# Gathered-row products behind the U chunk and behind the V chunk of each step

## The chip, the cores and the metric

The kernel runs on one core of a Trainium2 chip. The time is that of one execution on the device in microseconds (us); of several executions the median is taken. The engines are TensorE (PE in the profile; PEld is its weight load), VectorE (DVE), ScalarE (ACT), GpSimd (POOL) and SyncE (SP, used here only to issue transfers). Each works through its own queue in order.

## The reference

One layer of a decoder over 512 tokens of width 1024: layer norm, a mixer of state-space heads and latent attention, layer norm, then a product-key expert layer ("PEER"), and a last layer norm. Only the expert layer matters here. For each token it picks 128 of 16384 experts (8 heads x 16) and gives each a gate; then

```python
u = jnp.take(u_table, expert_idx, axis=0)
act = jax.nn.gelu(jnp.einsum('td,thkd->thk', xb, u).astype(jnp.float32), approximate=False)
v = jnp.take(v_table, expert_idx, axis=0)
return jnp.einsum('thk,thkd->td', (gate * act).astype(xb.dtype), v)
...
h = layer_norm(DEEPNORM_ALPHA * h + ffn, ln_ffn_g[l], ln_ffn_b[l])
```

Everything is float32.

## The kernel before

**Two ways through the expert layer.** For the first 384 tokens the kernel doesn't gather: it multiplies all 16384 experts with all tokens and lets a matrix of gates, zero where an expert wasn't picked, select. The tables are cut into 128 chunks of 128 experts. (For 64 of the 384 the first half is done by gathering too, earlier, and comes in ready.) The last block of 128 tokens is gathered: for each of the 128 picks s of a token one indirect transfer on POOL brings 128 rows, one per token (512 KB), of the u table, and VectorE multiplies them with the token's vector and sums (the *product* of step s < 128, line 1548); after GELU and gate (lines 1550 and 1552) the same is done with the v table, where VectorE adds the scaled row to a sum (128 <= s < 256, line 1554). So 256 products run on VectorE beside the matmuls of the other tokens.

**U chunk and V chunk.** `u_chunk` (line 1413; `u_half`, line 1395) computes the 320 activations of one chunk: 24 matmuls (line 85 to 87: high x high, high x low, low x high halves of the float32 values), then GELU on ScalarE into `ACT` (line 1406). `v_chunk` (line 1674) first makes the low half `Pl` of the next chunk's weights (`v_lo`, line 1659), prepares the chunk after next (`v_prep`: one quarter of a gate load on SP, line 1595; activations times gates, line 1628 on VectorE, or copies on ScalarE, lines 1631 and 1632), splits off its high half `Ph` (line 1651), and runs 18 matmuls into six accumulators (lines 1668, 1669, 1672).

**The stream of tables.** Both kinds of chunk take a 512 KB weight tile from one stream, `win` (class `Stream`, line 93), in turn U, V, U, V. An `item()` for chunk n of the stream emits, for the chunk n + 3, the high half on ScalarE (`wih`, every fourth in a buffer of its own, `wihx`; line 122), for n + 2 the low half on VectorE (`wil`, line 132), and behind that the load of the raw tile n + 5 on SP (line 104), which takes the buffer that this low half has just read. There are three raw buffers.

**The order of the work** is written out by hand (line 1698 on). A *step* is one turn of this loop. For `vc` 0 to 8 a step holds a V chunk alone; for `vc` 9 to 52 it holds a U chunk (`uc` 84 to 127) and a V chunk; for 53 to 120 again a V chunk alone. The last seven V chunks are kept for the end.

**Dealing out the products.** `gather` (line 1517) is a generator; each turn fetches the row of s + 4 on POOL and emits product s on VectorE, and notes s in `GS[0]`. There are five row buffers, so the row of s + 4 takes the buffer of product s - 1. At the end of each step the loop works out `want`, the count of products that should stand by then, from the units of chunk work that are left (`units`, line 1696: a V chunk is 0.86, a U and a V chunk together 2), and pumps the generator until it is reached (lines 1715 to 1719). `GS[1]` and `GS[2]` hold the units and the count when this began, in step 0. So on VectorE a step with both chunks is: `wil` for the next U chunk, `Pl`, line 1628 where there is one, `wil` for the next V chunk, then three or four products.

Of the kernel before, what the change touches and what calls it, by code (L numbers as in the profile page):

```python
# [46 lines left out]
T_U = 3.6  # L47
T_Q = 6.3
ROWS = 5
ENDU = 11  # L50
GP = 4
WV = 0.86
GST = (1, 3, 5, 7)
LOWA = (*range(2, 32, 2), 34, 38)
# [12 lines left out]
def tile_block(ctx: ExitStack, tc: tile.TileContext, I, out):  # L67
# [6 lines left out]
    def pool(name, bufs=1, **kw):  # L74
        p = tc.alloc_tile_pool(name=name, bufs=bufs, **kw)
        opened.append(p)
        return p
# [11 lines left out]
    def chain(*gs):  # L89
        for g in gs:  # L90
            yield from g
# [188 lines left out]
    def item():  # L280
        cnt[0] += 1
        return win.get(cnt[0] - 1)
# [749 lines left out]
    def stage1(m):  # L1032
        yield top16(sc.pop(m), 128, TV4[:, :, m], TI4[:, :, m])
        h = m // 2
        if m % 2:
            cand = rt.tile([128, NB, 88], F32, name="cand")
            for c0, a0, na, w in ((0, 0, 1, 16), (16, 1, 3, 8), (40, 4, 12, 4)):
                sh = [128, NB, na, w]
                (V if m == 15 else G).tensor_tensor(
                    cand[:, :, c0:c0 + na * w].rearrange("p h (a b) -> p h a b", a=na),  # L1040
                    TV4[:, :, m - 1, a0:a0 + na, None].to_broadcast(sh),
                    TV4[:, :, m, None, 0:w].to_broadcast(sh), op=OP.add)
            late_c.append((cand, h))
        if late_c and (m % 2 == 0 or m == 15):
            cand, h = late_c.pop()
            yield (0.7 if m == 15 else 0.0) + top16(cand, 88, TS4[:, :, h], PO4[:, :, h])
# [267 lines left out]
    def pump(g, us):  # L1314
        bal[0] = min(bal[0] + us, us)
        while bal[0] > 0:
            c = next(g, None)
            if c is None:
                bal[0] = 0.0
                return False  # L1320
            bal[0] -= c
        return True
# [61 lines left out]
    def refill():  # L1384
        while away:
            t = act_tile()
            if t is None:
                return
            c = away.pop(0)
            G.dma_start(t, asp[c - KEEP])  # L1390
            ACT[c] = t
# [21 lines left out]
    def u_chunk(c, psum=None):  # L1413
        for e in range(2):
            u_half(c, e, psum)
# [54 lines left out]
    fill = iter(())  # L1470
    for m in range(17):
# [6 lines left out]
        if m:  # L1478
            fill = chain(fill, stage1(m - 1))
# [35 lines left out]
    GS = [-1, 0, 0]  # L1515

    def gather():
        close(ijp)
        x3 = UR["x3"]
        gp3 = pool("gp3", side="right")  # L1520
        gp2 = pool("gp2", side="right")
        gp4 = pool("gp4", side="right")
        row = lambda s: (gp2 if s % ROWS < 3 else gp4).tile([128, D], F32, name="row", bufs=3 if s % ROWS < 3 else ROWS - 3)
        hd = gp3.tile([128, 128], F32, name="hd")
        ac = gp2.tile([128, D], F32, name="ac")
        V.tensor_scalar(wide(ac), x3, ALPHA, None, op0=OP.mult)
        R = {}
        yield 0.1

        def fetch(s):  # L1530
            if s < 256:
                R[s] = row(s)
                G.indirect_dma_start(out=R[s], out_offset=None, in_=I["u"] if s < 128 else I["v"],  # L1533
                                     in_offset=bass.IndirectOffsetOnAxis(ap=ix3[:, s % 128:s % 128 + 1], axis=0))
        for s in range(ROWS - 1):
            fetch(s)
            if s == 1:
                yield 0.0
            if s == 2:
                yield 0.0  # L1540
        for s in range(256):
            GS[0] = s
            if s == 0:
                yield 3.4
            fetch(s + ROWS - 1)
            r = R.pop(s)
            if s < 128:
                V.scalar_tensor_tensor(wide(r), wide(r), 1.0, x3, op0=OP.mult, op1=OP.mult, accum_out=hd[:, s:s + 1])  # L1548
                if s == 127:
                    A.activation(hd, hd, AF.Gelu)  # L1550
                    yield 0.2
                    V.tensor_tensor(hd, hd, g3, op=OP.mult)
            else:
                V.scalar_tensor_tensor(ac, r, hd[:, s - 128:s - 127], ac, op0=OP.mult, op1=OP.add)  # L1554
            yield 1.2
        R2 = [row(s) for s in (256, 257)]
        for i in range(2):
            row1(R2[i], 4 + i)
        yield 1.2
        mv, rs = norm_stats(gp3, ac, "lg")  # L1560
        yield 2.2
        V.scalar_tensor_tensor(ac, ac, mv[:, 0:1], R2[0], op0=OP.subtract, op1=OP.mult)
        yield 1.2
        V.scalar_tensor_tensor(ac, ac, rs, R2[1], op0=OP.mult, op1=OP.add)
        G.dma_start(out[3 * 128:, :], ac)
        yield 1.2
        close(gp4, gp2, gp3)
# [3 lines left out]
    fill = gather()  # L1571
# [19 lines left out]
    def step_g():  # L1591
        if more_g:
            q, b0, b1 = more_g.pop(0)
            m = min(b1, b0 + GP)
            nc.sync.dma_start(gt[q][:, b0:m], gsp[b0:m, :, q * 4:q * 4 + 4, :].rearrange("b j i t -> j b i t"))
            if m < b1:
                more_g.insert(0, (q, m, b1))
            elif more_g and m - b0 + more_g[0][2] - more_g[0][1] <= GP:
                step_g()
# [19 lines left out]
    def v_prep(c):  # L1619
        load_g(c // 4)  # L1620
        if c % 4 == 0:
            load_g(c // 4 + 1)
        step_g()
        a = ACT.pop(c)
        P = vst.tile([128, NT], F32, name="P", bufs=2)
        nb = open_(c)
        if nb:
            V.tensor_tensor(P[:, :nb * 32].rearrange("p (b t) -> p b t", t=32), a[:, :nb * 32].rearrange("p (b t) -> p b t", t=32),  # L1628
                            gt[c // 4][:, :nb, c % 4, :], op=OP.mult)
        if nb < ND:  # L1630
            A.activation(P[:, nb * 32:NU], a[:, nb * 32:], AF.Copy)
        A.activation(P[:, NU:].rearrange("p (b t) -> p b t", t=32), gt[c // 4][:, ND:, c % 4, :], AF.Copy)
        if c % 4 == 3:
            gt.pop(c // 4)
        prepared[0] += 1
        return P
# [11 lines left out]
    def v_hi(c, P):  # L1648
        Ph = v_sb(c, "Ph")
        for t, a, b in Ph:  # L1650
            A.activation(t, P[:, a:b], AF.Copy)  # L1651
        pend.append((c, P, Ph))

    def v_lo():
        if pend:
            c, P, Ph = pend.pop()
            Pl = v_sb(c, "Pl")
            for (t, a, b), (h, _, _) in zip(Pl, Ph):
                V.tensor_tensor(t, P[:, a:b], h, op=OP.subtract)  # L1659
            blk = lambda z: [t[:, i:i + 128] for t, a, b in z for i in range(0, b - a, 128)]  # L1660
            PP[c] = (blk(Ph), blk(Pl))
# [12 lines left out]
    def v_chunk(c):  # L1674
        v_lo()
        P = v_prep(c + 2)
        if uc == 128:
            v_hi(c + 2, P)
        hl = item()
        if uc < 128:  # L1680
            v_hi(c + 2, P)
        for b in range(3):
            v_mm(b, c, hl)
# [11 lines left out]
    more = True  # L1695
    units = lambda: (128 - uc) * 2 + WV * (uc - vc)
    fin = None
    while vc <= LASTC:
        w = 1.0
        if uc == 128 and not win.place:  # L1700
            i0 = len(items) - 127 + LASTC
            xv = [XT[:, 2 * j:2 * j + 2].rearrange("p a b -> p (a b)") for j in range(8)]
            win.place = {i0 + j: (xv[2 * j], xv[2 * j + 1]) for j in range(4)}
        refill()
        if uc < 128 and vc >= GAP:
            u_chunk(uc)
            uc += 1
            w = 2.0
        v_chunk(vc)
        vc += 1  # L1710
        if GS[0] < 0:
            more = pump(fill, 2.1 * w)
        else:
            if not GS[1]:
                GS[1:] = units() - ENDU, GS[0]
            left = units()
            want = 253 - max(0.0, (256 - GS[2]) * (left - ENDU) / GS[1])
            while more and GS[0] < want:
                more = pump(fill, 0.1)
            if more and left < ENDU:  # L1720
                more = pump(fill, 1.8)
            if not more and fin is None:
                fin = pool("fin", side="right")
                R2 = fin.tile([128, 2, D], F32, name="R2")
                for i in range(2):
                    row1(R2[:, i], 4 + i)
                xr = [fin.tile([128, D], F32, name=f"xr{b}") for b in range(3)]
                for b in range(3):
                    G.dma_start(xr[b], xsp[b])
# [141 lines left out]
```

## Time and profile before

| | us |
|---|---|
| median of 3 executions | 1562.88 (1562.26 to 1566.12) |
| the profiled execution | 1566.67 |
| its span, first to last instruction | 1564.9 |
| VectorE, products of the u table (line 1548) | 151.2, 128 of 1.22 |
| VectorE, products of the v table (line 1554) | 163.9, 128 of 1.28 |
| VectorE, low halves (line 132) | 282.3, 234 of 1.21 |
| POOL, row fetches (line 1533) | 181.5 and 206.0, 128 each |

The second part of the page cuts the span into 40 equal slices; each digit is the busy share of a slice in tenths:

```profile
PE   9999999999999999999999999999999999999997
DVE  8989767746799999999997687888889999999997
POOL 0000032510145433444431555665656676755610
DMA  6342122474322567999998999999999999999984
```

A slice is 39 us. The products begin in slice 23 of 40 (881 us) and end in slice 39 (1508 us). From there on VectorE and the transfers are as full as TensorE, nearly; which of them holds the others up has to be read from the waits. A wait in the profile is idle time of an engine, put down to what ended it.

### The profile page before, as it was taken

How to read it: one execution, taken by the hardware profiler on the slowest of the kernel's cores; microseconds unless marked ns; L12 is line 12 of the kernel's file. 1: busy time of each engine (PE TensorE's matmuls, PEld its weight loads, DVE VectorE, ACT ScalarE, POOL GpSimd, SP SyncE). 2: the span in 40 equal slices, each digit the busy share in tenths (PEclk: the TensorE clock that was granted, in tenths of full speed). 3: DMA queues.
4: the chain of work that ended last, by engine and by line, in shares of the span. 5: the costliest groups of instructions: out<-in, count | busy, mean ns of one | idle time of the engine just before them, and what ended most of it. 6: DMA issues, size and time to landing. Idle time of an engine off the chain costs nothing.

```text
span 1564.9 us, 24551 instructions
## 1 busy us (share of the span) xinstructions
PE 1531.6 (98%) x8696; PEld 1340.0 (86%) x8696; DVE 1354.9 (87%) x2610; ACT 755.2 (48%) x1412; POOL 631.3 (40%) x467
## 2 busy tenths in 40 slices
PE   9999999999999999999999999999999999999997
PEld 7787888888888999999989798898888878888886
DVE  8989767746799999999997687888889999999997
ACT  5575467732333446666666434444443434444342
POOL 0000032510145433444431555665656676755610
PEclk9999999999999999999999999999999999999999
DMA  6342122474322567999998999999999999999984
GB/s 249 100 155 89 56 75 53 122 245 160 125 89 88 153 217 234 347 322 367 348 319 301 357 354 345 365 386 369 376 378 383 395 390 382 388 377 366 370 293 151
DMA packets 153227, 416.22 MB, mean 266 GB/s; under 512 B 15440, under 2 KB 56400, under 8 KB 152848
## 3 DMA queue, kind: packets, MB, share of 16 engines
q1 hardware_dynamic: 94848, 209.29, 38.6%
q0 software_dynamic: 52384, 186.68, 32.8%
q10 hardware_dynamic: 5872, 18.68, 3.1%
q8 instruction: 68, 1.11, 0.3%
q14 instruction: 55, 0.45, 0.1%
HBM read 382.90 MB, written 29.59 MB: 264 GB/s over the span
## 4 chain that ended last, share of the span: by engine, by line
PE 49%; DVE 15%; DMA 14%; issue 13%; POOL 6%; ACT 3%; DVEq 0%; POOLq 0%; ACTq 0%
PE va L1668 8%; PE va L1672 8%; PE va L1669 8%; DMA row<-u,ix 5%; DMA urow<-u,uix 3%; POOL row L1533 3%; PE pa L87 3%; PE pa L86 3%; PE pa L85 3%; POOL urow L1136 3%; PE pu L85 2%; PE pu L87 2%; PE pu L86 2%; DMA wir<-ut 2%; DMA row<-v,ix 2%
## 5 line engine op out<-in xcount | busy, mean ns | idle before, releaser
L122 ACT ACTIVATE wih<-wir 128x1024 fp32r<-128x1024 f32 (+2 forms) x269 | 277.6, 1033 | 294.6 <-DMA wir<-v 143.7
L132 DVE TENSOR_TENSOR wil<-wir,wih 128x1024 fp32r<-128x1024 f32 (+1 forms) x234 | 282.3, 1209 | 67.9 <-ACT wih L122 55.9
L87 PE MATMUL pu<-XT,wil 128*128 128x320 f32 x1008 | 313.2, 311 | 5.9 <-DVE wil L132 5.7
L1669 PE MATMUL va<-wil,Ph 128*128 128x512 f32 x726 | 283.7, 391 | 0.0
L1533 POOL DMA_INDIRECT row<-v,ix x128 | 206.0, 1609 | 120.2 <-DVE ac L1554 96.5
L1668 PE MATMUL va<-wih,Ph 128*128 128x512 f32 x612 | 239.0, 391 | 2.3 <-ACT Ph L1651 2.3
L1533 POOL DMA_INDIRECT row<-u,ix x128 | 181.5, 1418 | 114.3 <-DVE row L1548 87.1
L85 PE MATMUL pu<-XT,wih 128*128 128x320 f32 x664 | 208.3, 314 | 2.9 <-ACT aout L1409 2.8
L86 PE MATMUL pu<-XT,wih 128*128 128x320 f32 x664 | 205.1, 309 | 0.0
L87 PEld LDWEIGHTS pu<-XT,wil 128*128 128x128 f32 x1008 | 189.2, 188 | 9.9 <-DVE wil L132 9.8
L1672 PE MATMUL va<-wih,Pl 128*128 128x512 f32 x612 | 189.6, 391 | 1.2 <-DVE Pl L1659 1.2
L1548 DVE SCALAR_TENSOR_TENSOR row<-row,XT 128x1024 f32<-128x1024 f32 x128 | 151.2, 1220 | 21.3 <-DMA row<-u,ix 21.1
L1554 DVE SCALAR_TENSOR_TENSOR ac<-row,hd,ac 128x1024 f32<-128x1024 f32 x128 | 163.9, 1281 | 3.6 <-DMA row<-v,ix 1.7
L1669 PEld LDWEIGHTS va<-wil,Ph 128*128 128x128 f32 x726 | 136.6, 188 | 27.3 <-DVE wil L132 0.3
L1136 POOL DMA_INDIRECT urow<-u,uix x64 | 102.4, 1600 | 133.3 <-DVE urow L1142 119.5
L1672 PEld LDWEIGHTS va<-wih,Pl 128*128 128x128 f32 x612 | 115.2, 188 | 26.0 <-DVE Pl L1659 1.7
L1668 PEld LDWEIGHTS va<-wih,Ph 128*128 128x128 f32 x612 | 115.3, 188 | 25.1 <-ACT Ph L1651 2.5
L132 POOL TENSOR_TENSOR wil<-wir,wih 128x1024 fp32r<-128x1024 f32 (+3 forms) x35 | 72.8, 2088 | 153.7 <-PE pw L87 99.3
L1651 ACT ACTIVATE Ph<-P 128x384 fp32r<-128x384 f32 x121 | 62.8, 519 | 140.6 <-DVE P L1628 102.8
L85 PEld LDWEIGHTS pu<-XT,wih 128*128 128x128 f32 x664 | 124.6, 188 | 5.1 <-ACT aout L1409 3.4
L86 PEld LDWEIGHTS pu<-XT,wih 128*128 128x128 f32 x664 | 124.7, 188 | 0.9
L85 PE MATMUL pu<-XT,wihx 128*128 128x320 f32 x344 | 107.5, 312 | 1.3 <-ACT aout L1409 0.9
(509 smaller groups left out, 3328.6 us busy)
## 6 DMA issues: line engine op xcount, KB each, us to landing
wir<-ut SPq DMA_DIRECT2D x128, 512.0 KB, 6.7
wir<-v SPq DMA_DIRECT2D x128, 512.0 KB, 6.7
gt<-gsp SPq DMA_DIRECT2D x63, 256.0 KB, 8.2
wir<-wo SPq DMA_DIRECT2D x26, 512.0 KB, 3.9
gsp<-stg ACTq DMA_DIRECT2D x21, 448.0 KB, 6.9
wir<-wf SPq DMA_DIRECT2D x18, 512.0 KB, 3.4
wir<-wqr SPq DMA_DIRECT2D x16, 512.0 KB, 3.7
asp<-aout SPq DMA_DIRECT2D x29, 160.0 KB, 6.1
```

The source lines that it names most:

```text
L85: T.matmul(ps, lh, rh, start=start, stop=False)
L86: T.matmul(ps, lh, rl, start=False, stop=False)
L87: T.matmul(ps, ll, rh, start=False, stop=stop)
L122: A.activation(h, r, AF.Copy)
L132: self.lo(n).tensor_tensor(l, r, h, op=OP.subtract)
L1136: G.indirect_dma_start(out=UR[n], out_offset=None, in_=I["u"], in_offset=bass.IndirectOffsetOnAxis(ap=UR["ix"][:, n:n + 1], axis=0))
L1533: G.indirect_dma_start(out=R[s], out_offset=None, in_=I["u"] if s < 128 else I["v"], in_offset=bass.IndirectOffsetOnAxis(ap=ix3[:, s % 128 ...
L1548: V.scalar_tensor_tensor(wide(r), wide(r), 1.0, x3, op0=OP.mult, op1=OP.mult, accum_out=hd[:, s:s + 1])
L1554: V.scalar_tensor_tensor(ac, r, hd[:, s - 128:s - 127], ac, op0=OP.mult, op1=OP.add)
L1668: T.matmul(va[b][e], Ph[b], h[:, cs], start=c == 0, stop=False)
L1669: T.matmul(va[b][e], Ph[b], l[:, cs], start=False, stop=False)
L1672: T.matmul(va[b][e], Pl[b], h[:, cs], start=False, stop=c == 127)
```

## The change

The working out of `want` and the pumping become a function, `dots_to`, which is called in a step with both chunks right behind the U chunk and again behind the V chunk. After the U chunk the units that are left have fallen by 1.14, after the V chunk by another 0.86. Steps with a V chunk alone do what they did. The line `GP = 4` moves among the constants and keeps its value.

```diff
 ROWS = 5
+GP = 4
 ENDU = 11
-GP = 4
...
+    def dots_to():
+        if not GS[1]:
+            GS[1:] = units() - ENDU, GS[0]
+        want = 253 - max(0.0, (256 - GS[2]) * (units() - ENDU) / GS[1])
+        more = True
+        while more and GS[0] < want:
+            more = pump(fill, 0.1)
+        return more
+
     while vc <= LASTC:
...
             u_chunk(uc)
             uc += 1
             w = 2.0
+            if GS[0] >= 0 and more:
+                more = dots_to()
         v_chunk(vc)
         vc += 1
         if GS[0] < 0:
             more = pump(fill, 2.1 * w)
         else:
-            if not GS[1]:
-                GS[1:] = units() - ENDU, GS[0]
-            left = units()
-            want = 253 - max(0.0, (256 - GS[2]) * (left - ENDU) / GS[1])
-            while more and GS[0] < want:
-                more = pump(fill, 0.1)
-            if more and left < ENDU:
+            more = more and dots_to()
+            if more and units() < ENDU:
                 more = pump(fill, 1.8)
```

## The prediction

> **What bounds the kernel now.** I read the busy times first, then a table of stretches, then the waits between engines, then the order of time.
>
> ```profile
> PE 1531.6 (98%) x8696; PEld 1340.0 (86%) x8696; DVE 1354.9 (87%) x2610; ACT 755.2 (48%) x1412; POOL 631.3 (40%) x467
> ...
> core 0: us, PE busy (x) PEld busy (x) DVE busy (x) ACT busy (x) POOL busy (x), PEclk, DMA share, GB/s
> 904.02:1248.23 344.21, 338.93 (x1849) 303.49 (x1848) 302.74 (x424) 141.57 (x252) 210.58 (x148) 1.00 0.99 372
> 1248.23:1262.60 14.37, 12.99 (x56) 9.90 (x54) 14.26 (x18) 5.36 (x11) 9.80 (x7) 1.00 1.03 396
> 1262.60:1508.30 245.70, 245.70 (x1085) 203.46 (x1084) 235.90 (x275) 102.87 (x185) 149.06 (x89) 1.00 1.03 378
> 1013.45:1066.79 53.34, 53.34 (x296) 48.26 (x295) 46.76 (x73) 22.38 (x39) 34.19 (x25) 1.00 1.01 386
> ```
>
> TensorE is the bound over the whole span. The first stretch is the 44 steps that hold a U chunk and a V chunk (1849 matmuls, 24 + 18 a step); only these are changed. The fourth stretch is seven of them in a row without a stall: 53.34 / 7 = 7.62 us a step. Forty-four such steps would take 335.3; they take 344.2, so **8.9 us** are lost there. (The busy column shows only 5.3 of it, since overlapping matmuls hide short gaps.) The next stretch is the first three steps with a V chunk alone: 14.37 against 3 x 245.70 / 60 = 12.3 (the third stretch holds 1085 / 18 = 60 V chunks), **2.1 us** lost. In the third stretch TensorE is never idle. So 11.0 us of the span is all that this change can win, unless it reaches work that it doesn't touch.
>
> What TensorE waits for there:
>
> ```profile
> ACT wih L122 <- DMA wir<-v: 127.5, 39, 6.2
> ...
> DVE row L1548 <- DMA row<-u,ix: 21.1, 17, 2.5
> ...
> DVE wil L132 <- ACT wih L122: 11.5, 13, 1.7
> ...
> PE pu L87 <- DVE wil L132: 5.0, 9, 0.9
> ...
> 989.68 0.31 PE L86 MATMUL pu<-XT,wihx 128*128 128x320 f32 x1
> 990.47 0.41 PE L87 MATMUL pu<-XT,wil 128*128 128x320 f32 x1 [0.48 <-DVE wil L132]
> ...
> 993.80 0.39 PE L1668 MATMUL va<-wih,Ph 128*128 128x512 f32 x1
> ...
> 1254.77 0.50 PE L1672 MATMUL va<-wih,Pl 128*128 128x512 f32 x1 [1.24 <-DVE Pl L1659]
> ```
>
> Columns of the waits: us in total, times, longest. It is always the U chunk (pu) that waits for its low half wil, never the V chunk; and, after the last U chunk, a V chunk that waits for Pl. VectorE (DVE) stands idle 21.1 us for gathered rows and 11.5 us for high halves. In order of time:
>
> ```profile
> 977.09 1.22 DVE L1548 SCALAR_TENSOR_TENSOR row<-row,XT 128x1024 f32<-128x1024 f32 x1
> ...
> 979.38 1.22 DVE L132 TENSOR_TENSOR wil<-wir,wih 128x1024 fp32r<-128x1024 f32 x1
> 980.52 0.55 DVE L1659 TENSOR_TENSOR Pl<-P,Ph 128x384 fp32r<-128x384 f32 x1
> 981.29 1.23 DVE L132 TENSOR_TENSOR wil<-wir,wih 128x1024 fp32r<-128x1024 f32 x1 [0.22 <-ACT wih L122]
> 982.43 1.22 DVE L1548 SCALAR_TENSOR_TENSOR row<-row,XT 128x1024 f32<-128x1024 f32 x1
> 983.58 0.08 DVE L1548 DVE_READ_ACCUMULATOR row<-row,XT 128x1 f32 x1
> 983.58 1.22 DVE L1548 SCALAR_TENSOR_TENSOR row<-row,XT 128x1024 f32<-128x1024 f32 x1
> ...
> 988.05 1.22 DVE L1548 SCALAR_TENSOR_TENSOR row<-row,XT 128x1024 f32<-128x1024 f32 x1 [2.10 <-DMA row<-u,ix]
> 989.20 0.08 DVE L1548 DVE_READ_ACCUMULATOR row<-row,XT 128x1 f32 x1
> 989.20 1.22 DVE L132 TENSOR_TENSOR wil<-wir,wihx 128x1024 fp32r<-128x1024 f32 x1
> 990.34 0.55 DVE L1659 TENSOR_TENSOR Pl<-P,Ph 128x384 fp32r<-128x384 f32 x1
> 990.80 1.22 DVE L132 TENSOR_TENSOR wil<-wir,wih 128x1024 fp32r<-128x1024 f32 x1
> 991.94 1.22 DVE L1548 SCALAR_TENSOR_TENSOR row<-row,XT 128x1024 f32<-128x1024 f32 x1
> ...
> 995.38 1.22 DVE L132 TENSOR_TENSOR wil<-wir,wih 128x1024 fp32r<-128x1024 f32 x1
> ...
> 979.42 1.99 POOL L1533 DMA_INDIRECT row<-u,ix  x1 [0.30 <-issue]
> ```
>
> A step on VectorE is wil for U, Pl, wil for V, then a lump of products. Here a lump of four (982.43 to 989.20), whose last product waits 2.10 us for its row; then wil for U, which TensorE already wants. The next lump has three. From one start to the next a product takes 1.15, a wil 1.14, Pl 0.46. A step of three is 995.38 - 989.20 = 6.18 us of work, one of four 7.33: 13.5 for two, against 15.24 of TensorE. VectorE has the time; it loses it by waiting, and catches up too little in between.
>
> **The change, part by part.** The pacing (line 1717) gives 256 / 148.4 = 1.725 products per unit, 148.4 being (128 - 84) x 2 + 0.86 x 83 - 11 when it starts. A U chunk is 2 - 0.86 = 1.14 units, or 1.97 products; a V chunk 0.86, or 1.48. So two products (once only one) now stand behind U and one or two behind V; each step still ends at the same count. No instruction is added or removed. The moved constant has the same value and costs nothing. Three things move against each other:
>
> 1. Pl, the product with gates (line 1628) and wil for V come two products later in VectorE's queue. Wil for the next U has the same work ahead of it as before. Price: 2 x 1.15 = 2.3 us of V's slack. At 990.80 wil for V ends 1.8 us ahead of its chunk (993.80), and its first use is the second matmul. So if VectorE stays as late as it is, V chunks wait 0.3 to 0.5 us; if it gets 0.5 us ahead, nothing.
>
> 2. Rows. A row is fetched when the fifth product before it has freed its buffer. The product at 988.05 uses the buffer of the one at 977.09: from that one's end (978.3) to the landing 9.7 us passed, 1.1 of it because its fetch (979.42) stood behind another on POOL. At TensorE's pace the time from a product's end to the start of the fifth after it is, for seven products of a pair of steps, before: 7.6, 7.6, 8.8, 8.8 and three times 11.8; after: 7.6, 9.2 and five times 10.2 to 10.4. (Sum of the work between them, plus the 1.4 us that a step of three leaves free; the pair that waits above goes from 8.8 to 10.4.) Most of the 21.1 us should go.
>
> 3. Loads. Each wil frees the buffer for a load three chunks on: wil of U releases V's load, wil of V releases U's.
>
> ```profile
> wir<-v SPq DMA_DIRECT2D x45, 512.0 KB, 6.6
> wir<-ut SPq DMA_DIRECT2D x41, 512.0 KB, 7.3
> ...
> L122 ACT ACTIVATE wih<-wir 128x1024 fp32r<-128x1024 f32 x68 | 72.2, 1061 | 172.5 <-DMA wir<-v 127.5 <-DMA wir<-ut 27.3 <-PE va L1669 11.9
> L1554 DVE SCALAR_TENSOR_TENSOR ac<-row,hd,ac 128x1024 f32<-128x1024 f32 x37 | 47.5, 1283 | 2.6 <-DMA row<-v,ix 1.7
> L1628 DVE TENSOR_TENSOR P<-act,gt 128x320 f32<-128x320 f32 x14 | 6.8, 483 | 0.0
> ```
>
> V's load and split need 6.6 + 1.06 + 0.1 = 7.8 us; from wil of U to the next step's wil of V there are 7.62 + 0.46 = 8.1: 0.3 to spare, which is why VectorE meets unfinished high halves. After: 10.4. U's need 7.3 + 1.06 + 0.1 = 8.5; from wil of V to the wil of U two steps on there are now some 11.6, after 7.62 + 1.15 or 2.3 = 8.8 or 9.9. U's load becomes the tight one, by 0.3 us in one step of two; being late there it delays a split that stands after it, and the pair still has 1.7 us free. I price this at nothing to 1 us in all.
>
> On POOL the fetches keep their order and there is nothing else behind the V chunk; on SP the gate load stands between the two weight loads as before, and V's wil releases the second 2.3 us later. ScalarE's part is unchanged.
>
> The last nine steps have the dearer product (1.28) and line 1628 (0.48, of which 0.4 shows): 2 x 1.14 + 0.46 + 0.4 + 3.45 x 1.28 = 7.6 a step, no slack. They live on whatever lead VectorE has won before; with a lead of 2 us they and the three steps behind them don't stall.
>
> **The sum**, against the profiled execution (1566.67 = span 1564.9 + 1.8): of 11.0 us lost I leave 1.5 in the 44 steps (the one short row time in seven, U's load, the last nine) and 1.0 behind them: -8.5, so 1558.2. The median is 1562.88, 3.8 lower. If those 3.8 us were all in these stalls, 7.2 are left in an ordinary run and 5.6 can go; if none, 8.5. I take 7: **1556**. Its own range is 1552 (all gone) to 1558.
>
> **The rivals.**
>
> *Only the first part works*: the steps up to 1178 stop stalling, but VectorE enters the last nine without a lead, and the V chunks there wait, 2.3 to 2.6 us of slack being gone. Of the 11.0 about 4.5 remain more than forecast: 1560. For it: no slack in those nine. Against: the 13.5 of 15.24 in the 35 before.
>
> *The stall moves from U to V*: VectorE's waits stay as long, TensorE runs in step with VectorE, and only the chunk that waits is another. A period that VectorE sets doesn't change: 1563. For it: the 0.3 to 0.5 us worked out above. Against: two causes of the waits lose their reason.
>
> *Transfers are the bound*: if the DMA engines carried no more than the 372 GB/s of this stretch, fewer waits on VectorE would become longer ones: 1563. At 335.3 us the stretch needs 372 x 344.2 / 335.3 = 382. Against: the seven steps without a stall moved 386. The Trainium skill, "DMA: Bandwidth & Descriptors", section "Where 436 GB/s comes from", speaks for it: it has HBM bind transfers into SBUF at about 358 GB/s per core, by which this stretch is full already and nothing can be won. The trace doesn't agree here: 386 and 396 in the rows above.
>
> *Slower*: in a step of three the second product, now ahead of Pl and V's wil, still has only 7.6 us for its row. If it takes the 9.7 us seen above, the pair can't be shorter than that plus the work outside, 9.7 + 6.2 = 15.9, and 16.3 with line 1628, against 344.2 / 22 = 15.65 now; 22 pairs by 0.25 to 0.65 are 5 to 14 us: about 1572. It decides from 9.4 us. Against: in the kernel before, the same pair of products has the same bound and no wait in the rows above; the long time belonged to the product whose fetch queued.
>
> **Chances.** Forecast 0.56; only the first part 0.13; stall moved 0.14; transfers 0.08; slower 0.09. A run can tell about 0.3% (4.7 us) from no change: faster is below 1558.2, slower above 1567.6. So faster 0.56, same 0.13 + 0.14 + 0.08 = 0.35, slower 0.09. The range reaches from 1552 through the cases that change little, to 1564; what it leaves out is the slower case and the edges.
>
> **What would show it.** Right: the 44 steps take 337 us or less; the wait of L87 for wil is gone; rows on L1548 wait under 8 us in all; wil for V never meets an unfinished high half; in each step on VectorE stand wil, two products, Pl, wil, one or two. The stall has moved if V's first low-half matmul (L1669) or L1672 shows waits for wil or Pl. Transfers bind if GB/s stays at 372 while waits on DMA stay. It would be slower by long row waits ahead of Pl. What would make me wrong most simply: longer landings of U's load, or a lead that VectorE doesn't keep.

## The result and the profile after

The changed kernel takes 1553.7 us (median of 6, 1551.38 to 1556.01), the kernel before 1566.34 in the same comparison (6 runs, 1562.26 to 1568.42): a ratio of 0.9931, 95% interval 0.9911 to 0.995. (The ratios and intervals here are those on record for each comparison, not quotients of the medians; the medians alone give 0.9919 here.) Later, on another chip, it was 1554.0 against 1564.25, ratio 0.9922 (0.9899 to 0.9945). The forecast was 1556 with 1552 to 1564, faster.

The profiled execution of the changed kernel took 1553.19 us (span 1551.4). The table of stretches, with the 44 steps first and the first three steps with a V chunk alone behind them (columns as before: start, end and length, then busy time of PE, PEld, DVE, ACT and POOL, clock, DMA share, GB/s):

```profile
900.80:1236.08 335.28, 335.28 (x1849) 303.34 (x1848) 306.07 (x426) 145.21 (x254) 217.58 (x151) 1.00 1.01 386
1236.08:1248.59 12.51, 12.51 (x57) 10.28 (x55) 10.95 (x14) 4.21 (x8) 8.11 (x5) 1.00 1.04 395
```

344.21 became 335.28, which is 44 x 7.62 to the hundredth: TensorE doesn't stall once. VectorE's busy time is the same as before but for 3.3 us (302.74, now 306.07, a few of its operations having moved into the stretch); what went is its idle time. The second row runs to the second matmul of the fourth V chunk (1248.59); from its first matmul at 1236.08 to the fourth chunk's at 1248.36 the three chunks take 12.28, where they took 14.37.

The stretch also begins 3.22 us earlier (900.80 for 904.02). That isn't the change's: the order of the work up to there is the same in both kernels. Of it 1.6 us lie in the nine V chunks ahead, which took 38.4 us in two profiles of the kernel before and in one with the new order, and 36.9 in four with the new order and one with the old (the one without row fetches). So of the 13.5 us between the two profiled executions 10.3 are the change's: 8.9 in the stretch and the rest in the five V chunks behind it (2.1 us lost before, 0.8 now).

The waits from 900 to 1251 us, which is this stretch with the V chunks behind it (us in total, times, longest; in the stretch alone the first line is 51.5, 32 times, and the others are the same):

```profile
ACT wih L122 <- DMA wir<-v: 53.0, 34, 3.1
...
DVE wil L132 <- issue: 11.9, 11, 1.3
...
DVE row L1548 <- DMA row<-u,ix: 5.3, 10, 1.0
DVE wil L132 <- ACT wih L122: 4.3, 5, 1.9
DVE wil L132 <- ACT wihx L122: 4.1, 5, 1.7
```

Rows are waited for 5.3 us instead of 21.1, high halves 8.4 instead of 11.5; no wait of L87 for wil is left. What has grown is `wil <- issue`, 3.8 before. "issue" is idle time for which the profile names no releaser; the order of time shows what it is:

```profile
984.42 1.23 DVE L132 TENSOR_TENSOR wil<-wir,wih 128x1024 fp32r<-128x1024 f32 x1 [1.28 <-issue]
985.57 1.22 DVE L1548 SCALAR_TENSOR_TENSOR row<-row,XT 128x1024 f32<-128x1024 f32 x1
986.71 0.08 DVE L1548 DVE_READ_ACCUMULATOR row<-row,XT 128x1 f32 x1
986.71 1.22 DVE L1548 SCALAR_TENSOR_TENSOR row<-row,XT 128x1024 f32<-128x1024 f32 x1
987.86 0.08 DVE L1548 DVE_READ_ACCUMULATOR row<-row,XT 128x1 f32 x1
987.86 0.56 DVE L1659 TENSOR_TENSOR Pl<-P,Ph 128x384 fp32r<-128x384 f32 x1
988.39 1.23 DVE L132 TENSOR_TENSOR wil<-wir,wih 128x1024 fp32r<-128x1024 f32 x1
989.53 1.22 DVE L1548 SCALAR_TENSOR_TENSOR row<-row,XT 128x1024 f32<-128x1024 f32 x1
...
992.04 1.22 DVE L132 TENSOR_TENSOR wil<-wir,wihx 128x1024 fp32r<-128x1024 f32 x1
...
992.24 0.30 PE L85 MATMUL pu<-XT,wih 128*128 128x320 f32 x1
...
992.53 0.31 PE L87 MATMUL pu<-XT,wil 128*128 128x320 f32 x1
```

The order is the forecast one: wil, two products, Pl, wil, one or two. But the wil at 992.04 isn't the one that the U chunk of 992.24 uses; that one was made at 984.42, 6.6 us (985.65 to 992.24) ahead. VectorE now runs a whole step ahead, and starts a wil just as TensorE begins a chunk, since only then does one of the three buffers for it come free. Its idle time is a wait for room, which costs nothing.

### The profile page after: what moved, and what is told of

It reads as the page before. It is cut to its first block, busy times and chain, and to the rows that moved or that the text cites. A ratio compares the mean times of both kernels' runs of the same rounds, so it can differ in the third digit from the quotient of the medians.

```text
span 1551.4 us, 24602 instructions
## 1 busy us (share of the span) xinstructions
PE 1525.2 (98%) x8696; PEld 1338.7 (86%) x8696; DVE 1354.9 (87%) x2610; ACT 758.6 (49%) x1412; POOL 640.9 (41%) x467
## 4 chain that ended last, share of the span: by engine, by line
PE 85%; DVE 7%; ACT 3%; DMA 3%; issue 1%; ACTq 0%; DVEq 0%; SPq 0%; POOLq 0%
PE va L1669 11%; PE va L1672 11%; PE va L1668 11%; PE pu L85 9%; PE pu L87 9%; PE pu L86 9%; PE pa L86 3%; PE pa L87 3%; PE pa L85 3%; PE pw L86 3%; PE pw L87 3%; PE pw L85 3%; DVE wil L132 1%; PE pw L1271 1%; PE pw L1272 1%
## 5 line engine op out<-in xcount | busy, mean ns | idle before, releaser
L87 PE MATMUL pu<-XT,wil 128*128 128x320 f32 x1008 | 311.6, 309 | 0.4 <-DVE wil L132 0.4
L1669 PE MATMUL va<-wil,Ph 128*128 128x512 f32 x726 | 283.1, 390 | 0.0
L1533 POOL DMA_INDIRECT row<-v,ix x128 | 217.2, 1697 | 112.4 <-DVE ac L1554 88.1
L87 PEld LDWEIGHTS pu<-XT,wil 128*128 128x128 f32 x1008 | 189.2, 188 | 0.7 <-DVE wil L132 0.7
L1669 PEld LDWEIGHTS va<-wil,Ph 128*128 128x128 f32 x726 | 136.3, 188 | 27.0
```

The source lines that it names most:

```text
L87: T.matmul(ps, ll, rh, start=False, stop=stop)
L1669: T.matmul(va[b][e], Ph[b], l[:, cs], start=False, stop=False)
```

## The experiments

Two theories stood against each other for what the lump had cost. *Rows*: the last product of a lump of four waits for its row, and wil for U stands behind it. *Loads*: wil for U and wil for V stood side by side, so that the V load had only 0.3 us to spare. A third, *order*, needs neither: four products are too much work ahead of wil, whatever they wait for. Each kernel is read by its 44 steps; "lost" is their time less 335.3.

| kernel | 44 steps | lost | VectorE waits for rows (u + v) | for high halves | lost in the 5 V chunks behind |
|---|---|---|---|---|---|
| before | 344.2 | 8.9 | 21.1 + 1.7 | 11.5 | 2.1 |
| before, again | 346.3 | 11.0 | 20.1 + 3.2 | 14.9 | 3.6 |
| changed | 335.3 | 0.0 | 5.3 + 0.6 | 8.4 | 0.8 |
| changed, again | 336.6 | 1.3 | 1.5 + 1.8 | 7.2 | 1.1 |
| control (KEEP 52) | 346.7 | 11.4 | 20.8 + 4.5 | 13.0 | 2.4 |
| control, six row buffers | 338.2 | 2.9 | 1.4 + 0 | 15.9 | 4.0 |
| control, four raw buffers | 342.5 | 7.2 | 25.7 + 4.8 | 0 | 4.4 |
| changed (KEEP 52) | 335.5 | 0.2 | 5.2 + 0.4 | 5.0 | 1.4 |
| one product behind U | 335.3 | 0.0 | 12.9 + 2.2 | 1.6 | 0.0 |
| all behind U | 349.7 | 14.4 | 13.8 + 0 | 29.7 | 0.8 |
| before without row fetches | 335.3 | 0.0 | 0 | 0 | 0.0 |
| changed, WV 0.75 | 341.5 | 6.2 | 9.7 + 0.7 | 8.3 | 1.2 |

### More room for rows, or for loads

The kernel before has no memory left for a sixth row or a fourth raw buffer, so three activation tiles were taken away first; that is the control.

```diff
-KEEP = 55
+KEEP = 52
```

> The kernel before with KEEP at 52 instead of 55: three activation tiles (3.75 KB per partition) less, so that the two kernels beside it have room; steps with a U chunk then begin at vc 12 instead of 9. It is their control. Both theories: the 44 steps with U and V chunk lose 7 to 11 us over 335.3 as in the kernel before (8.9), rows are waited for on L1548 for 15 to 25 us, and the whole is within 4 us of the kernel before.

It lost 11.4 us in the 44 steps and took 1567.88 us, ratio 1.0033 (1.0015 to 1.005) to the kernel before (1563.09 in this comparison): 4.8 us more, where up to 4 were expected.

```diff
-ROWS = 5
+ROWS = 6
```

> The control with six row buffers instead of five; order of products, loads of the tables and raw buffers as in the control. Each row then has one product more, 1.15 us or a lump gap, to arrive. Theory 'rows' (a lump of four waits for its last row, and that makes wil for U late): the row waits fall below 6 us and the 44 steps lose under 2.5 us. Theory 'loads' (the V load has only 0.3 us to spare, since wil of U and wil of V stand close together): the row waits fall, but the 44 steps still lose 6 us or more. Theory 'order' (four products ahead of wil for U are too much work at a time, whatever they wait for): still 6 us or more. Both rows and loads: 2.5 to 6.

```diff
-    win = Stream(wst, "wi", items, [128, 1024], raw=3, la=2, lo=lambda n: lo_on[0])
+    win = Stream(wst, "wi", items, [128, 1024], raw=4, la=2, lo=lambda n: lo_on[0])
```

> The control with four raw buffers instead of three in the stream of tables; rows and order of products as in the control. Each table load then has one chunk more to arrive. Theory 'rows': the 44 steps still lose 6 us or more, and the row waits stay at 15 us or more. Theory 'loads': VectorE's waits for high halves go from 11.5 to under 4 us and the 44 steps lose under 2.5 us. Theory 'order': 6 us or more. Both rows and loads: 2.5 to 6. Other stretches of the kernel get the fourth buffer too, so its whole time may fall for other reasons; the 44 steps are what is read.

> The changed kernel with KEEP at 52. All theories of the change: the 44 steps lose under 1.5 us as in the changed kernel (0.0), and the time lies 8 to 13 us below the control's. If it loses more than 4 us, the gain hangs on where the steps begin, not on the dealing out.

The 44 steps of the control, and its waits:

```profile
913.08:1259.73 346.65, 339.05 (x1850) 303.38 (x1848) 303.68 (x423) 141.31 (x249) 213.53 (x150) 1.00 1.00 372
...
DVE row L1548 <- DMA row<-u,ix: 20.8, 15, 3.1
...
DVE wil L132 <- ACT wih L122: 9.3, 9, 1.5
PE pu L87 <- DVE wil L132: 7.5, 12, 1.4
```

With six row buffers (the second row is its first 33 steps and a quarter of the next):

```profile
912.60:1250.75 338.15, 336.60 (x1850) 303.32 (x1849) 304.10 (x423) 141.65 (x247) 217.83 (x150) 1.00 1.00 380
912.60:1166.00 253.40, 253.40 (x1401) 229.45 (x1400) 224.91 (x342) 109.08 (x193) 169.53 (x113) 1.00 1.00 379
...
DVE wil L132 <- ACT wih L122: 11.2, 9, 2.5
...
DVE row L1548 <- DMA row<-u,ix: 1.4, 2, 1.1
PE pu L87 <- DVE wil L132: 1.3, 3, 0.7
```

With four raw buffers:

```profile
912.90:1255.37 342.47, 337.46 (x1849) 303.43 (x1848) 303.42 (x423) 144.49 (x249) 210.31 (x149) 1.00 0.99 373
...
DVE row L1548 <- DMA row<-u,ix: 25.7, 23, 3.4
...
PE pu L87 <- DVE wil L132: 4.8, 6, 1.5
```

The sixth row buffer alone, lumps and load chain as they were, takes the loss from 11.4 to 2.9, and all of that in the last eleven steps (the first 33 run at full pace). The fourth raw buffer takes VectorE's waits for high halves away altogether, and still 7.2 are lost, while the row waits grow. So rows are the larger cause, 8.5 of 11.4, and loads the smaller, 4.2. The two add to more than the whole; I take it that either gives VectorE time in which it meets the other's delay less, which isn't shown. The share of the loads is uncertain: with the V chunks behind, the control loses 13.8, six row buffers 6.9, four raw buffers 11.6, so that only 2.2 are the loads', about as much as two profiles of one kernel differ. By the bounds set beforehand the sixth row buffer falls just into "both" (2.9, from 2.5), and the fourth raw buffer into "rows" (7.2, from 6).

The changed kernel with KEEP at 52 lost 0.2 us and lies 10.7 us below the control (1557.23 against 1567.88). So the gain doesn't hang on where the steps begin.

Whole times: six row buffers 1557.64, ratio to the kernel before 0.9969 (0.9952 to 0.9986); four raw buffers 1561.16, 0.9989 (0.9973 to 1.0006). Six row buffers come out level with the changed kernel at the same KEEP (1557.23, 0.9975, 0.9961 to 0.9989), which needs no memory for its gain.

### How many behind U

One behind U, the rest behind V:

```diff
+    def dots_to(most=256):
...
+        want = min(want, GS[0] + most)
...
-                more = dots_to()
+                more = dots_to(1)
```

> The changed kernel with only one product behind each U chunk; the other two or three stay behind the V chunk. Time from a product's end to the start of the fifth after it, for seven in a row: 7.6, 8.8, 9.2 and four of 10.2 or more (changed kernel: 7.6, 9.2 and five of 10.2 or more; before: 7.6, 7.6, 8.8, 8.8 and three of 11.8). Theory 'rows' (with loads as the smaller part): row waits between the two kernels, 6 to 14 us, and 0 to 3 us lost in the 44 steps. If the number behind U has to be two for another reason, 5 us or more are lost.

All behind U:

```diff
+    def dots_to(d=0.0):
...
-        want = 253 - max(0.0, (256 - GS[2]) * (units() - ENDU) / GS[1])
+        want = 253 - max(0.0, (256 - GS[2]) * (units() - d - ENDU) / GS[1])
...
-                more = dots_to()
+                more = dots_to(WV)
```

> The changed kernel with all three or four products behind the U chunk and none behind the V chunk. Lumps as before, so row waits of 15 us or more by theory 'rows'. The V load gets 11 us and more; but wil of V and wil of the next U now stand side by side, so that the U load has only one step, 7.6 us, for the 8.5 us that its 7.3 us landing and its split need. If loads bind like that, VectorE waits for high halves of U on most steps and the 44 steps lose 10 to 39 us; if the load chains matter little, the loss is 6 to 12 us as in the kernel before and only the chunk that waits is another (V).

> The changed kernel once more, on another chip, against the kernel before. All theories: the 44 steps take 335 to 337 us, and the median lies 7 to 13 us below that of the kernel before (ratio 0.992 to 0.9955).

One behind U:

```profile
900.50:1235.78 335.28, 335.28 (x1850) 303.34 (x1848) 307.44 (x429) 147.04 (x256) 213.51 (x151) 1.00 1.01 388
...
DVE row L1548 <- DMA row<-u,ix: 12.9, 20, 2.7
```

All behind U:

```profile
898.17:1247.89 349.72, 339.96 (x1849) 304.11 (x1848) 306.00 (x427) 143.48 (x254) 209.34 (x151) 1.00 0.99 372
...
DVE wil L132 <- ACT wih L122: 15.0, 10, 3.2
DVE wil L132 <- ACT wihx L122: 14.7, 12, 2.2
DVE row L1548 <- DMA row<-u,ix: 13.8, 12, 1.8
...
PE va L1669 <- DVE wil L132: 9.5, 9, 1.9
```

With one behind U nothing is lost either, though rows are waited for 15.1 us (a little over what was expected): 1553.72 us, ratio 0.9934 (0.9914 to 0.9954), beside the 0.9922 of the changed kernel in the same comparison. So row waits aren't a price by themselves. VectorE has some 32 us to spare in 335: in the kernel before it was busy 302.74 of the 344.21. What counts is whether its waits leave it ahead. With all behind U they don't: 14.4 us are lost, and the chunk that waits is now V's (L1669). Its waits for high halves, 29.7 us, all stand at wil for U: it is the U load whose time is down to one step, 7.6 us for the 8.5 that it needs, as expected. The row waits, 13.8 us, stayed just under the 15 expected; with one behind U about as much row wait cost nothing. 1567.25 us, ratio 1.0018 (0.9998 to 1.0037): moving the products all the way gives back everything that dealing them out wins.

### The order alone

```diff
-        R = {}
+        R, base = {}, {}
...
         def fetch(s):
-            if s < 256:
-                R[s] = row(s)
+            if s >= ROWS - 1:
+                R[s] = base[s % (ROWS - 1)]
+            else:
+                R[s] = base[s] = row(s)
...
+        scr = row(ROWS - 1)
...
-                V.scalar_tensor_tensor(wide(r), wide(r), 1.0, x3, op0=OP.mult, op1=OP.mult, accum_out=hd[:, s:s + 1])
+                V.scalar_tensor_tensor(wide(scr), wide(r), 1.0, x3, op0=OP.mult, op1=OP.mult, accum_out=hd[:, s:s + 1])
```

> The kernel before without the row fetches: only the first four rows are gathered, all 256 products run on those (the last block's result is left wrong by that; the work of VectorE is the same). No product waits for a row, and the transfers have room. Theory 'order' (four products at a time ahead of wil for U are too much for VectorE, whatever they wait for): the 44 steps still lose 6 us or more. Theories 'rows' and 'loads': under 1 us, or up to 2 in the last nine steps, where VectorE's own work fills the step.

```profile
900.32:1235.60 335.28, 335.28 (x1850) 303.36 (x1848) 312.40 (x429) 143.85 (x255) 0.00 (x0) 1.00 0.51 151
```

Lumps of three and four as before, VectorE as busy as ever (312.40 us), and not a stall, in the last nine steps neither; its one execution took 1551.9 us. The order of VectorE's work alone costs nothing; "order" is out. It doesn't tell rows from loads, since without the fetches the loads land sooner too (last section).

### Again, and more products in these steps

> The kernel before once more, for a second profile of it. All theories: the 44 steps lose 7 to 12 us (8.9 in the first profile), the row waits are 18 to 25 us; what lies ahead of the first U chunk of these steps may differ by up to 4 us between executions and says nothing of the change.

The 44 steps in the second profile of the kernel before and in that of the changed kernel:

```profile
900.27:1246.59 346.32, 338.49 (x1850) 303.46 (x1848) 301.49 (x423) 141.12 (x250) 213.72 (x148) 1.00 0.99 369
900.39:1236.97 336.58, 335.85 (x1849) 303.28 (x1848) 304.97 (x425) 144.14 (x252) 211.60 (x150) 1.00 1.01 383
```

The kernel before lost 11.0 us in the 44 steps and 3.6 behind: its first profile was on the low side. The changed one lost 1.3 and 1.1.

```diff
-WV = 0.86
+WV = 0.75
```

> The changed kernel with WV at 0.75: a V chunk counts for less, so more products fall into the steps with both chunks (161 instead of 152 in the 44; two or three behind U, one or two behind V) and fewer into the V chunks alone. Bytes moved in the 44 steps go from 386 x 335.3 to 9 x 524 KB more, 400 GB/s at full pace. If transfers bind near the 386 to 396 GB/s that stretches without a stall have shown, the 44 steps take 339 us or more and waits on DMA grow well beyond 15 us. If they have room, the steps lose under 3 us (VectorE's own work is over the pace in the last steps), and the V chunks behind them lose nothing. The whole time: within 3 us of the changed kernel in the second case.

The 44 steps in two parts, 33 and 11, and what TensorE waits for:

```profile
900.36:1151.81 251.45, 251.45 (x1387) 227.52 (x1386) 229.60 (x347) 110.30 (x193) 163.76 (x118) 1.00 1.02 393
1151.81:1241.85 90.04, 85.76 (x464) 75.56 (x462) 86.49 (x88) 34.60 (x60) 63.66 (x41) 1.00 1.01 382
...
PE va L1669 <- DVE wil L132: 4.3, 7, 1.3
```

Thirty-three steps at full pace with 393 GB/s: the transfers have room. But 6.2 us are lost, in neither of the two ways expected: all in the last eleven steps, where VectorE is busy 86.49 of 90.04 us; at TensorE's pace the eleven take 83.8, less than that work. There the products are those of the v table, line 1628 is at its dearest, and 3.66 products a step are more than VectorE can do. 1563.69 us, ratio 0.999 (0.9973 to 1.0007): some 10 us above the 1553.7 and 1554.0 of the changed kernel, where at most 3 were expected. Moving products this way gives the gain back; a WV above 0.86 wasn't tried.

## Why the prediction was right, point by point

**What bounds the kernel.** Right: the stalls of these steps and of the V chunks behind them were what could be won, and nearly all of it was; 0.8 and 2.4 us are left in two profiles of the changed kernel. But 11.0 us was not "all that this change can win": it was the loss of one execution, and the second profile of the kernel before lost 14.6.

**1, V's slack.** The 2.3 us were paid, and hidden as said: VectorE got not 0.5 but some 6 us ahead. That there is a price where VectorE is not ahead is shown by all behind U, where L1669 waits, and by the second profile of the changed kernel, whose 1.3 us are V chunks in the last nine steps.

**2, rows.** Right, and the larger cause: "most of the 21.1 us should go", 5.3 and 1.5 are left; the sixth row buffer does the same without any dealing out. What I had not seen is that the remaining waits could be three times as long (15.1 us with one behind U) and still cost nothing.

**3, loads.** Right in the mechanism. V's load was tight: VectorE's waits for it (11.5 us) are gone. It is the smaller cause, of a size that stays uncertain. U's became the tight one: all ten waits for a high half that are left in the 44 steps of the changed kernel, and all five in its second profile, stand at wil for U, none at wil for V. It shows by the load that such a wil releases, which is V's:

```profile
1154.63 1.23 DVE L132 TENSOR_TENSOR wil<-wir,wih 128x1024 fp32r<-128x1024 f32 x1 [1.91 <-ACT wih L122]
...
1155.89 0.33 SPq L104 DMA_DIRECT2D wir<-v  x1
```

I had U's load late by 0.3 us in one step of two. It is late less often and by more, ten times by 0.8 us on average (1.9 at most) and five times by 1.4 (2.7 at most); why some loads are so late stays open. These waits came to 8.4 and 7.2 us and cost nothing in the first profile, being met by the lead. In the second, one of 2.42 us at 1203.56 stands ahead of the first stall of all (L1669 at 1209.36), so that some of the 1.3 us may be its price; this isn't shown. With all products behind U, where the same load is tightest, more than the whole gain was lost.

**The last nine steps.** Right: they live on the lead. Nothing was lost there in one profile, 1.3 us in the other.

**The sum.** This is the term that was mis-sized. I held 2.5 us back; the profiles show 0.8 (first) and 2.4 (second, 1.3 + 1.1). And I took 1.5 off for the median of three lying 3.8 below the profiled execution, as if an ordinary run had fewer stalls: with three more runs the median rose to 1566.34, and a second profile lost 11.0. So it was 7 us forecast, and 10.3 to 12.6 measured by medians; the two first profiles show 10.3, where 8.5 had been taken off the profiled execution. That 1553.7 came so near 1556 is in part luck: the median it started from was 3.5 us lower than that of the six runs, the gain was put 5.6 us too small, and the two errors partly cancel.

**The rivals.** *Only the first part works* and *the stall moves* didn't happen, though the second is what all behind U does. *Transfers are the bound* is answered by 386 GB/s over the whole stretch and 393 over 251 us in a variant, without a stall; the bound of the Trainium skill ("DMA: Bandwidth & Descriptors", section "Where 436 GB/s comes from"), about 358, doesn't hold for this stream on this chip. *Slower*: the row waits come to 5.3 us in ten places, 1.0 at most, so the pair with 7.6 us for its row doesn't wait the 2 us that this case needed.

## What to carry to other kernels

When a filler on a shared in-order engine waits for transfers, look at when each transfer is released, not only at how much work the filler is: dealing it out evenly gives every buffer about the same time to be filled, which was worth as much here as another buffer (0.0 us lost by dealing out, 2.9 by a sixth row buffer). An engine with a tenth of its time to spare can still set the pace, if a wait and a full lump fall in front of the same deadline. And such a filler should be spread, not just moved: put entirely behind the other chunk it took the time from the other load.

## What the runs showed of the hardware that was not expected

Without the row fetches a 512 KB load lands in little more than half the time (median us from issue to landing; the 44 steps of that kernel, at 151 GB/s):

```profile
wir<-v SPq DMA_DIRECT2D x47, 512.0 KB, 3.6
wir<-ut SPq DMA_DIRECT2D x41, 512.0 KB, 4.2
```

Beside the fetches, at 372 GB/s, it was 6.6 and 7.3. The load chain that had 0.3 us to spare is tight because of its neighbours, and one that is planned by the landing time of a load without them would be planned 3 us too short.
